# Row normalization on one core: the last scale is shared by two engines in both tiles, and the last store is issued on the ScalarE queue

## Chip, cores, metric

One Trainium2 chip, one core. The metric is device microseconds of a whole execution. All runs quoted here were in the fast state (granted clock 1.0); one program on one core.

## The reference

```python
def reference(x, axis, eps):          # x: (1024, 4096) float32, axis -1, eps 1e-12
    norm = np.sqrt(np.sum(x ** 2, axis=axis, keepdims=True) + eps)
    return (x / norm).astype(np.float32)
```

16.78 MB are read and 16.78 MB written; the arithmetic per element is one square, one add and one multiply.

## The kernel before

Each of two tiles holds 4 rows in each of 128 partitions (64 KiB per partition, contiguous in HBM). Both loads are issued at the start; each store follows its tile's scales. What the change and the argument touch:

```python
    def scale(self, r):
        self.nc.vector.tensor_scalar_mul(
            out=self.x[:, r], in0=self.x[:, r], scalar1=self.rstd[:, r : r + 1]
        )

    def scale_by_both(self, r):
        cut = 7 * self.D // 8
        rstd = self.rstd[:, r : r + 1]
        self.nc.scalar.activation(
            out=self.x[:, r, :cut], in_=self.x[:, r, :cut], func=ACT_F.Copy, scale=rstd,
        )
        self.nc.vector.tensor_scalar_mul(
            out=self.x[:, r, cut:], in0=self.x[:, r, cut:], scalar1=rstd
        )
# ... cut ...
    for i in range(n_tiles):                                   # n_tiles = 2
        g = RowGroups(nc, io, stats, scratch, D, R, eps_t)
        load = nc.sync.dma_start(out=g.flat(), in_=x_t[i])
        # ... cut: the first load is moved to the front ...
    for i, g in enumerate(groups):
        # ... cut: squares, norms and scales of rows 3, 0, 1; square of row 2 ...
        g.norm(2)
        if i < n_tiles - 1:
            g.scale_by_both(2)
        else:
            g.scale(2)
        store = nc.sync.dma_start(out=out_t[i], in_=g.flat())
    gpsimd_waits_for_last_store(nc, store.ins)
```

## Time and profile before

| | before |
|---|---|
| time, median (lowest to highest) | 81.92 us (81.86 to 81.96), 3 runs |
| profiled span | 80.2 us |
| VectorE / ScalarE busy | 26.7 / 29.7 us |
| DMA engines busy | 97.4% of the span, one queue |
| last store issued / landed | 56.76 / 80.03 us |

How to read it: a share near 100% on the DMA line and under 40% on the engines says that the end is set by bytes, not by arithmetic. To see whether a later or earlier issue matters, compare the issue time with the time at which the engines run out of the work queued ahead of it. The page and its stretches, timeline and chain are shown and read in the prediction below.

In the table of stretches, a DMA packet is counted whole, time and bytes, in the stretch in which it starts. So for a short stretch in which each of the 16 engines starts exactly one packet, "DMA share x length" is the mean duration of that packet, and "GB/s x length" is 1.05 MB (16 x 64 KiB). For the first packets of the last store, in the kernel before (columns: stretch, length, busy time and count of VectorE, ScalarE and GpSimd, clock, DMA share, GB/s):

```profile
59.70:60.40 0.70, 0.00 (x0) 0.00 (x0) 0.00 (x0) 1.00 3.47 1498
```

1498 x 0.70 = 1049 KB, all sixteen; 3.47 x 0.70 = 2.43 us per packet. The packet records themselves (start and duration of each) say 2.42.

### The profile page before, as it was taken

The page shows a single profiled execution, that of the slowest core. Times are in us where ns is not written, and L with a number is a line of the kernel's source. Part 1 is how long each engine was busy: PE and PEld are TensorE (multiplying, and loading weights), DVE is VectorE, ACT ScalarE, POOL GpSimd, SP SyncE. Part 2 cuts the span into 40 slices and gives each one's busy share as a digit, 9 for nine tenths or more (in the row PEclk, how much of TensorE's full clock was granted, in tenths as well). Part 3 has the DMA queues.
Part 4 walks back from the last instruction along what each step waited for, and adds up shares of the span by engine and source line. Part 5 has one row for each costly group of instructions (what it writes and reads, how often), then busy time and mean ns, then how long its engine had stood idle before and what let it go on. Part 6 is the DMA issues. An engine that isn't in the chain of part 4 may idle for free.

```text
span 80.2 us, 93 instructions
## 1 busy us (share of the span) xinstructions
DVE 26.7 (33%) x21; ACT 29.7 (37%) x23; POOL 0.2 (0%) x4
## 2 busy tenths in 40 slices
DVE  0000000000099599960039995999200000000000
ACT  6000000000099999989439999950000000000000
POOL 0000000000000000000000000000000000000000
DMA  9099996699996699996699990999991999992990
GB/s 490 33 523 523 523 490 294 261 523 523 523 490 261 294 523 523 523 490 261 294 523 523 523 490 33 523 523 523 523 458 65 523 523 523 523 425 98 523 523 0
DMA packets 576, 33.55 MB, mean 418 GB/s; under 512 B 64, under 2 KB 64, under 8 KB 64
## 3 DMA queue, kind: packets, MB, share of 16 engines
q1 hardware_dynamic: 576, 33.55, 97.4%
HBM read 16.78 MB, written 16.78 MB: 418 GB/s over the span
## 4 chain that ended last, share of the span: by engine, by line
DMA 51%; ACT 10%; DVE 9%; issue 0%
DMA xt<-in_x_dram 51%; ACT sq_act L33 9%; DVE xt L64 9%; ACT rstd L53 1%; DVE rstd L59 0%
## 5 line engine op out<-in xcount | busy, mean ns | idle before, releaser
L33 ACT ACTIVATE sq_act<-xt 128x4096 f32<-128x4096 f32 x6 | 21.7, 3609 | 22.4 <-DMA xt<-in_x_dram 22.4
L42 DVE SCALAR_TENSOR_TENSOR sq_dve<-xt 128x4096 f32<-128x4096 f32 x2 | 8.9, 4426 | 26.4 <-DMA xt<-in_x_dram 26.4
L64 DVE TENSOR_SCALAR xt<-xt,rstd 128x4096 f32<-128x4096 f32 x7 | 16.5, 2353 | 0.2
L72 ACT ACTIVATE xt<-xt,rstd 128x3584 f32<-128x3584 f32 x1 | 3.3, 3283 | 0.2 <-DVE rstd L59 0.2
L53 ACT ACTIVATE rstd<-ssq,eps_t 128x1 f32<-128x1 f32 x8 | 2.1, 290 | 0.1
L59 DVE RECIPROCAL rstd<-rstd 128x1 f32<-128x1 f32 x8 | 1.3, 160 | 2.5 <-ACT rstd L53 2.5
L33 ACT ACT_TABLE_LOAD x1 | 1.3, 1283 | 0.8 <-PEq L258 0.8
L53 ACT ACT_TABLE_LOAD x1 | 1.3, 1283 | 0.0
L33 ACT ACTIVATION_READ_ACCUMULATOR sq_act<-xt 128x1 f32 x6 | 1.1, 187 | 0.0
L78 DVE TENSOR_SCALAR xt<-xt,rstd 128x512 f32<-128x512 f32 x1 | 0.5, 487 | 0.0
L211 DVE MEMSET eps_t<- 128x1 f32 x1 | 0.1, 59 | 0.9 <-PEq L258 0.9
L42 DVE DVE_READ_ACCUMULATOR sq_dve<-xt 128x1 f32 x2 | 0.2, 83 | 0.0
L258 POOL MEMSET const-uint8-127<- 128x1 uint8 x1 | 0.1, 103 | 0.0
L258 POOL MEMSET const-bfloat16-1.0<- 128x1 bf16 x1 | 0.1, 102 | 0.0
L258 POOL MEMSET const-float32-0.0<- 128x1 f32 x1 | 0.1, 99 | 0.2 <-issue 0.2
L258 POOL MEMSET const-float32-1.0<- 128x1 f32 x1 | 0.1, 99 | 0.0
## 6 DMA issues: line engine op xcount, KB each, us to landing
xt<-in_x_dram SPq DMA_DIRECT2D x2, 31.3
out_dram<-xt SPq DMA_DIRECT2D x2, 22.5
```

The lines of the kernel that those rows point to most:

```text
L33: self.nc.scalar.activation(out=sq_a, in_=self.x[:, r], func=ACT_F.Square, accum_out=self.ssq[:, r : r + 1],)
L42: self.nc.vector.scalar_tensor_tensor(out=sq_v, in0=self.x[:, r], scalar=1.0, in1=self.x[:, r], op0=ALU.mult, op1=ALU.mult, accum_out=self ...
L53: self.nc.scalar.activation(out=self.rstd[:, r : r + n], in_=self.ssq[:, r : r + n], func=ACT_F.Sqrt, bias=self.eps_t,)
L59: self.nc.vector.reciprocal(out=self.rstd[:, r : r + n], in_=self.rstd[:, r : r + n])
L64: self.nc.vector.tensor_scalar_mul(out=self.x[:, r], in0=self.x[:, r], scalar1=self.rstd[:, r : r + 1])
L72: self.nc.scalar.activation(out=self.x[:, r, :cut], in_=self.x[:, r, :cut], func=ACT_F.Copy, scale=rstd,)
L78: self.nc.vector.tensor_scalar_mul(out=self.x[:, r, cut:], in0=self.x[:, r, cut:], scalar1=rstd)
L211: nc.vector.memset(eps_t, eps)
L258: nc = _bacc.Bacc("TRN2", target_bir_lowering=False, num_devices=1)
```

## The change

The intent, as far as the diff shows it: the same code for both tiles, with the last scale split between two engines, and the last store issued by the engine that has just finished the larger part of it.

```diff
-        if i < n_tiles - 1:
-            g.scale_by_both(2)
-        else:
-            g.scale(2)
-        store = nc.sync.dma_start(out=out_t[i], in_=g.flat())
+        g.scale_by_both(2)
+        queue = nc.sync if i < n_tiles - 1 else nc.scalar
+        store = queue.dma_start(out=out_t[i], in_=g.flat())
```

## The prediction

> **What bounds the kernel now.** I read the page's engine line and DMA rows first, then the busy table by stretches of time, then the timeline around the two stores, then the chain of work that ended last. All figures are of the kernel before; its span is 80.2 us, its time 81.92 us.
>
> The page's engine line, its rate row and its queue row:
>
> ```profile
> DVE 26.7 (33%) x21; ACT 29.7 (37%) x23; POOL 0.2 (0%) x4
> ...
> GB/s 490 33 523 523 523 490 294 261 523 523 523 490 261 294 523 523 523 490 261 294 523 523 523 490 33 523 523 523 523 458 65 523 523 523 523 425 98 523 523 0
> ...
> q1 hardware_dynamic: 576, 33.55, 97.4%
> ```
>
> No compute engine is busy for even 40% of the span, while the one DMA queue's packets fill 97.4% of what 16 DMA engines have. The ups and downs of the rate row are not pauses: a packet is counted whole in one slice. Of the 576 packets 64 are under 512 B (the completion marks), so 512 carry 64 KiB each, 32 per engine in turn: 8 for each of two loads and two stores. The queue's share gives about 0.974 x 80.2 x 16 / 512 = 2.44 us per packet; the DMA records of the trace say 2.42 us for nearly all of them, with about 2 ns between one packet of an engine and its next.
>
> The busy table by stretches, cut where a round of packets ends, shows the same (columns: stretch, its length, busy us and count of each engine, clock, DMA share, rate):
>
> ```profile
> 4.82:41.06 36.24, 12.45 (x10) 16.56 (x12) 0.00 (x0) 1.00 1.00 434
> 41.06:60.38 19.32, 14.23 (x10) 11.88 (x10) 0.00 (x0) 1.00 1.00 434
> 60.38:79.70 19.32, 0.00 (x0) 0.00 (x0) 0.00 (x0) 1.00 0.88 380
> 79.70:80.21 0.51, 0.00 (x0) 0.00 (x0) 0.00 (x0) 1.00 0.00 0
> ```
>
> The second stretch is store 0 draining, and all of tile 1's compute lies inside it. The third is store 1 draining, with no compute at all. (Its 0.88 is where packets are counted at their starts: the first ones of that store began just before the cut. 128 packets of 2.42 us over 16 engines are 19.36 us, the whole stretch.) The engine that starts last takes its first packet at 2.12 us and ends its last at 79.69: 77.57 us for 32 packets, 2.424 each. It never waits. The last landing is at 80.03 and the span ends at 80.20.
>
> So the end is set by 33.55 MB through 16 busy DMA engines, and the question for the change is only whether store 1 is ready before the engines run out of store 0. The timeline around the last scales and issues (start, us, engine, line):
>
> ```profile
> 35.48 0.16 DVE L59 RECIPROCAL rstd<-rstd 128x1 f32<-128x1 f32 x1 [0.57 <-ACT rstd L53]
> 35.68 3.28 ACT L72 ACTIVATE xt<-xt,rstd 128x3584 f32<-128x3584 f32 x1 [0.23 <-DVE rstd L59]
> 35.68 0.49 DVE L78 TENSOR_SCALAR xt<-xt,rstd 128x512 f32<-128x512 f32 x1
> 38.99 0.35 SPq L240 DMA_DIRECT2D out_dram<-xt  x1
> ...
> 54.18 0.16 DVE L59 RECIPROCAL rstd<-rstd 128x1 f32<-128x1 f32 x1
> 54.38 2.35 DVE L64 TENSOR_SCALAR xt<-xt,rstd 128x4096 f32<-128x4096 f32 x1
> 56.76 0.34 SPq L240 DMA_DIRECT2D out_dram<-xt  x1
> ```
>
> Tile 0 shows what the shared scale costs, tile 1 what the whole VectorE scale costs. Store 1 is issued at 56.76. In the DMA records, the sixteen engines finish store 0 between 59.79 and 60.37 and each goes on to store 1 2 ns later, so store 1 is already waiting. Lastly, the chain that ended last, whose final line is:
>
> ```profile
> 54.38 2.35 DVE xt L64
> ```
>
> It stops at 56.73, because this view follows compute and the final transfer has none behind it. The page's 9% for VectorE on this chain is therefore not time that can be won.
>
> **What the Trainium skill says.** "DMA: Bandwidth & Descriptors", section "Specifications", gives a fabric ceiling of 435 GB/s for the 16 engines. The trace agrees: 434 GB/s over the 55 us of stretches one and two. The same page, "Issuing engines are not separate DMA queues", says that DMAs from the scalar, sync or gpsimd engine run on the same 16 engines and interleave, and that issuing from several only saves sequencer time. Before, all issues are SyncE's, of 0.34 to 0.38 us each; no run yet shows ScalarE's. "ScalarE: Activation LUTs", section "Table sets: the hidden batching unit", says that cheap functions such as copy are filler in every set. The trace agrees: ScalarE's Copy at 35.68 follows Sqrt with no table load between them, and the only two loads are at 0.79 and 25.81.
>
> **The change, part by part.**
>
> 1. *The scale.* Removed: one VectorE scale of 128x4096, 2.353 us (54.377 to 56.730). Added: a VectorE scale of 128x512, 0.487 us, and a ScalarE Copy of 128x3584, 3.283 us, beside each other. Both need the reciprocal, which ends at 54.183 + 0.158 = 54.34. In tile 0 both began 0.035 us after it; here that gives 54.38. ScalarE is free by then (its last Sqrt ends at 53.34). VectorE's part ends at 54.38 + 0.49 = 54.86, ScalarE's at 54.38 + 3.28 = 57.66. The scale ends 57.66 - 56.73 = 0.93 us LATER than before. In tile 0 the split uses idle engines too, but the slow side gets seven eighths; it is no saving here.
>
> 2. *The issue.* Before, SyncE began its issue 0.027 us after VectorE's end (56.730 to 56.757). Now ScalarE waits for its own Copy; I take the same 0.03, so 57.69, an issue of about 0.35 us. ScalarE has nothing else to do, so its 0.35 us delays nothing. The order of the built kernel shows exactly these edits: ScalarE gains one Copy and one DMA, VectorE's last scale shrinks, SyncE loses one DMA, and no table load is added.
>
> 3. *From issue to the first byte.* Store 0 measures it: issued at 38.99, while the first engine had finished load 1 at 40.265 and stood idle until 40.475. So the first engine had its work 1.485 us after the issue, and the later ones by 40.67, 1.68 us after. For store 1: ready at 57.69 + 1.49 = 59.18 on the first engine, 57.69 + 1.68 = 59.37 on the last. The engines finish store 0 at 59.79 at the earliest. Slack before: 59.79 - (56.76 + 1.49) = 1.54 us. Slack after: about 0.6 us, or 0.4 by the slowest figure. [...]
>
> 4. *The transfer.* 128 packets of 2.42 us as before. With its own ring, store 1 may take turns with store 0's last packets from 59.2 on rather than line up behind them; the sum of bytes per engine is the same, so only store 0's landing (60.7 now) may shift, and nothing waits for it but a drain long before the end.
>
> 5. *The tail.* GpSimd waits for the last store's semaphore as before; 0.17 us from landing to end stays.
>
> Sum: +0.93 us (scale) - 0.93 us (absorbed in slack) + 0 (transfer) + 0 (tail) = 0. Predicted time 81.9 us.
>
> **The rivals.**
>
> *First, the slack does not hold (slower).* It needs an issue on ScalarE's own ring to take much longer than one on SyncE's. The very first load, with everything cold, needed 1.01 us for its first engine and 2.12 us for its last. Even 2.12 us gives 57.69 + 2.12 = 59.81, 0.02 us behind the earliest engine and before most of the others (the last needs it at 60.37). If the first DMA of ScalarE cost 1 us more than that, the loss would be about 0.5 us, 82.4. For 2% (1.64 us) it would have to be ready only at about 60.37 + 1.64 = 62.0, an issue-to-data time of over 4.3 us. Nothing in the profile speaks for that.
>
> *Second, two rings are better than one (faster).* If engines lost time at the seam between two stores on one ring, a second ring could fill it. Against it: the seam is 2 ns on every engine. And 434 GB/s over the whole middle leaves no hole for a second ring to fill. At most the 0.2 us hole at the load 1 to store 0 seam is in question, and the change doesn't touch that issue; the last engine doesn't have it either.
>
> *Third, two rings are worse.* Packets of two stores interleaving, or a second queue's set-up and clean-up around the kernel (81.92 - 80.2 = 1.7 us lie outside the profiled span), could cost some tenths: 82.1 to 82.4. No view of before can exclude this, since only one queue ran.
>
> **Range and chances.** The three runs before lie within 0.1 us, the profiled one took 82.04; another chip and the third rival add some tenths upward, and the second takes at most 0.3 off. So 81.6 to 82.4 for 8 in 10. Beyond 2% either way (under 80.3 or over 83.6) needs the DMA stream to shrink, which 77.57 us of unbroken packets forbid, or the over 4 us of issue latency: 1% for faster, 2% for slower.
>
> **What would show it right or wrong.** Right: the page shows a second queue with 144 packets and 8.39 MB beside 432 on the first, the two shares together near 97%; ScalarE's Copy at about 54.4 for 3.28 us; ScalarE's issue at about 57.7; the DMA share stays full through 59 to 61 us; the last landing at about 80.0. The chain of work ends with ScalarE's line, later than before, and the span doesn't move. Wrong: a hole in the DMA records around 60 us (the slack failed, step 3), packets other than 2.42 us while both queues have work (step 4), an unchanged span with a changed time (set-up of the second queue), or a last landing that moves for no hole at all.

## The result, and the profile after

The changed kernel took 82.72 us (82.59 to 82.83, 6 runs), the kernel before 81.93 us (81.73 to 81.96, 6 runs). The ratio is 1.0099, 95% interval 1.0085 to 1.0114: the mean time of one kernel's fast runs over that of the other's of the same rounds, so not quite the ratio of the medians. The change costs 0.8 us where the prediction had none. 82.72 lies above its range of 81.6 to 82.4 and clearly outside the noise; that the change would stay within 2% held.

The page's engine line, rate row and queue rows of the changed kernel:

```profile
DVE 24.9 (31%) x21; ACT 33.0 (41%) x24; POOL 0.2 (0%) x4
...
GB/s 518 0 518 518 518 518 486 97 453 518 518 518 486 162 389 518 518 518 518 0 518 518 518 518 453 130 453 518 518 518 0 518 518 518 518 130 389 518 518 0
...
q1 hardware_dynamic: 432, 25.17, 72.9%
q10 hardware_dynamic: 144, 8.39, 24.9%
```

VectorE lost 1.8 us and ScalarE gained 3.3, as foreseen. There is a second queue, q10, with the 128 large packets of the last store and its 16 marks. The queue rows already give the loss away. On q1, 0.729 x 80.9 x 16 / 384 = 2.46 us per large packet; on q10, 0.249 x 80.9 x 16 / 128 = 2.52. Eight packets per engine, each 0.1 us above 2.42 on average, are 0.8 us: the whole loss. (On q1 it is mostly the first packets of the first load that lift the mean.) The two shares still add up to 97.8%, so there is no idle hole; something took longer.

The timeline around the last scale and the issue, and the last line of the chain of work:

```profile
54.09 0.15 DVE L59 RECIPROCAL rstd<-rstd 128x1 f32<-128x1 f32 x1
54.28 0.49 DVE L78 TENSOR_SCALAR xt<-xt,rstd 128x512 f32<-128x512 f32 x1
54.28 3.28 ACT L72 ACTIVATE xt<-xt,rstd 128x3584 f32<-128x3584 f32 x1 [1.04 <-DVE rstd L59]
57.59 0.37 ACTq L238 DMA_DIRECT2D out_dram<-xt  x1
```

```profile
54.28 3.28 ACT xt L72
```

The compute side is as predicted: Copy at 54.28 for 3.28 us, issue at 57.59. The chain ends with ScalarE's line, at 57.56. The surprise is in the stretch where the engines pass from store 0 to the last store:

```profile
59.70:60.50 0.80, 0.00 (x0) 0.00 (x0) 0.00 (x0) 1.00 4.08 1311
```

Again all sixteen start here (1311 x 0.80 = 1049 KB), but 4.08 x 0.80 = 3.26 us each, against 2.43 before. In the packet records each of them starts 2 ns after the end of an engine's last packet of store 0, between 59.85 and 60.31, and lasts 3.07 to 3.48 us; the next round is back at 2.42. So each engine stood 0.65 to 1.06 us, 0.84 on average, "inside" its first packet of the new queue. Nothing else of that size differs: an engine's packets sum to 78.09 us on average before and to 79.14 after. Of this 1.05 us more, 0.84 lie in this round and about 0.2 in the last rounds of load 1 (2.46 to 2.50 us a packet; no other profile of the set has these long rounds, so they are this one execution's and not the change's). The first packets of all began 0.16 us earlier, which takes some of it back.

What could make it so? There were four theories:

- **Later scale**: the slack was not there after all; the 0.93 us later scale costs directly.
- **Cold queue**: the first use of ScalarE's queue is slow.
- **Slow issue**: a ScalarE issue always needs some 3.2 us until data flows (57.59 to 60.75).
- **Change of ring** (the "ring" of a queue is here the row of packets that it has waiting for an engine): passing from one queue's ring to the other's costs the engine a start-up, as if its pipeline had run empty. The first packets of the whole kernel have the same look (3.15 us on average in this run, against 2.42 in the round after), which is why I thought of it.

### The profile page after: what moved, and what is told of

It reads as the page before. It is cut to its first block, busy times and chain, and to the rows that moved or that the text cites. A ratio compares the mean times of both kernels' runs of the same rounds, so it can differ in the third digit from the quotient of the medians.

```text
span 80.9 us, 94 instructions
## 1 busy us (share of the span) xinstructions
DVE 24.9 (31%) x21; ACT 33.0 (41%) x24; POOL 0.2 (0%) x4
## 4 chain that ended last, share of the span: by engine, by line
DMA 50%; ACT 14%; DVE 6%; issue 0%
DMA xt<-in_x_dram 50%; ACT sq_act L33 9%; DVE xt L64 6%; ACT xt L72 4%; ACT rstd L53 1%; DVE rstd L59 0%
## 5 line engine op out<-in xcount | busy, mean ns | idle before, releaser
L64 DVE TENSOR_SCALAR xt<-xt,rstd 128x4096 f32<-128x4096 f32 x6 | 14.1, 2353 | 0.2
L72 ACT ACTIVATE xt<-xt,rstd 128x3584 f32<-128x3584 f32 x2 | 6.6, 3283 | 1.3 <-DVE rstd L59 1.3
L78 DVE TENSOR_SCALAR xt<-xt,rstd 128x512 f32<-128x512 f32 x2 | 1.0, 486 | 0.1
```

Source lines behind the costliest of these rows:

```text
L64: self.nc.vector.tensor_scalar_mul(out=self.x[:, r], in0=self.x[:, r], scalar1=self.rstd[:, r : r + 1])
L72: self.nc.scalar.activation(out=self.x[:, r, :cut], in_=self.x[:, r, :cut], func=ACT_F.Copy, scale=rstd,)
L78: self.nc.vector.tensor_scalar_mul(out=self.x[:, r, cut:], in0=self.x[:, r, cut:], scalar1=rstd)
```

## The experiments

The whole set, three rounds each, every result correct. The rounds ran on several chips, so the ratio, taken within the same rounds, says more than the time. "Issued" is the start of the last store's issue; "first packet" the mean of the 16 first packets of the last store.

| run | last store on | issued | first packet | time us | ratio to before |
|---|---|---|---|---|---|
| changed kernel | ScalarE | 57.59 | 3.26 | 82.72 | 1.010 |
| e1 scale only | SyncE | 57.6 | 2.42 | 81.90 | 0.999 |
| e2 queue only | ScalarE | 56.55 | 2.42 | 81.83 | 0.998 |
| e3 warmed queue | ScalarE | 57.45 | 3.26 | 82.76 | 1.010 |
| e4 both stores | ScalarE | 57.70 | 2.42 (store 0: 2.96) | 82.73 | 1.009 |
| e5 even split | ScalarE | 55.83 | 2.42 | 81.84 | 1.000 |
| e6 share 2816 | ScalarE | 56.85 | 2.90 | 82.41 | 1.007 |
| e7 share all | ScalarE | 57.76 | 3.26 | 82.67 | 1.010 |
| e8 late VectorE | ScalarE | 57.38 | 3.26 | 82.61 | 1.010 |
| e9 short last packet | ScalarE | 57.72 | 2.42 | 82.17 | 1.0035 |
| e10 its control | SyncE | 56.48 | 2.42 | 81.96 | 1.001 |
| e11 rings swapped | SyncE | 57.53 | 2.46 (store 0: 3.25) | 82.72 | 1.011 |
| e12 short first packet | ScalarE | 57.52 | 1.60 for 20 KiB | 82.73 | 1.010 |

### First four: halves of the change, a warmed queue, both stores

**e1**, the changed kernel with the store back on SyncE:

```diff
-        queue = nc.sync if i < n_tiles - 1 else nc.scalar
+        queue = nc.sync
```

> Only the shared last scale, last store still issued by SyncE. All theories that blame the new queue (first packet on a new ring is slow; ring switch costs; ScalarE's issue is slow to reach the engines) expect the time of the kernel before, about 81.9 us, with the last round-24 packets at 2.42 us, because the issue at about 57.7 plus 1.5 us still comes before 59.8. The rival that the 0.93 us later scale itself is what costs (the slack was not there) expects about 82.7 us and a hole in the DMA records near 60 us.

("Round 24" are the first packets of the last store, with rounds of sixteen counted from 0.) 81.90 us, ratio 0.9991 (0.9972 to 1.0009), first packets 2.70 x 0.90 = 2.43 us:

```profile
59.50:60.40 0.90, 0.00 (x0) 0.00 (x0) 0.00 (x0) 1.00 2.70 1165
```

The later scale is free, as the prediction's slack said. "Later scale" is out. In the records, the sixteen last packets of store 0 begin between 0.48 us before and 0.28 us after the issue at 57.61, much as in the changed kernel (0.16 before to 0.30 after). So at the same lateness every engine pays on the other ring and none on its own.

**e2**, the kernel before with the last store on ScalarE's queue:

```diff
-        store = nc.sync.dma_start(out=out_t[i], in_=g.flat())
+        queue = nc.sync if i < n_tiles - 1 else nc.scalar
+        store = queue.dma_start(out=out_t[i], in_=g.flat())
```

> Only the ScalarE queue; the last scale stays whole on VectorE, so ScalarE issues at about 56.8 instead of 57.6. Fixed cost theory (the first packet of each engine on a ring other than the last one takes 3.25 us instead of 2.42): 82.7 us, as the changed kernel. Readiness theory (a ScalarE issue needs about 3.2 us to data, seen as 57.6 to 60.8): data at about 60.0, so loss of at most 0.2 us, 82.0 us.

81.83 us, ratio 0.9984 (0.9968 to 0.9999). Each half of the change is free, and both together cost 0.8 us. The stretch of the first packets, and the issue:

```profile
56.55 0.37 ACTq L241 DMA_DIRECT2D out_dram<-xt  x1
```

```profile
59.50:60.30 0.80, 0.00 (x0) 0.00 (x0) 0.00 (x0) 1.00 3.04 1311
```

3.04 x 0.80 = 2.43 us: a change of ring at full speed. So the change of ring alone is not the cost either, nor is it a fixed price. What differs from the changed kernel is that the issue came one microsecond earlier.

**e3**, the changed kernel with a small DMA on ScalarE's queue at the start:

```diff
+    warm = scratch_pool.tile([16, 128], F32)
+    nc.scalar.dma_start(out=warm, in_=x[0:16, 0:128])
```

> The changed kernel plus one tiny DMA (16 rows of 512 B, 8 KB, read and never used) issued by ScalarE at the start. Cold-ring theory (only the first use of ScalarE's ring is slow): the last store's first packets take 2.42 us and the time falls to about 81.9 to 82.0. Switch theory (any change of ring on an engine empties the pipeline): the last store still pays 0.84, and the tiny DMA may pay once more, 82.7 to 83.5.

82.76 us, first packets 3.26 us (4.09 x 0.80 in its stretch): "cold queue" is out. The small DMA brought something better than its purpose. Its row among the DMA issues:

```profile
warm<-in_x_dram ACTq DMA_DIRECT2D x1, 8.0 KB, 8.9
```

8 KB took 8.9 us to land. In the packet records, on every engine, it ran between the second and the third packet of load 0 (from 6.40 us on), although it was issued at 0.78, 0.2 to 0.5 us before the first packets began. And it ran without any gap: 27 ns for its 512 B, and the next packet of load 0 began at once. An engine seems to settle its next packet one packet ahead.

**e4**, both stores on ScalarE:

```diff
-        queue = nc.sync if i < n_tiles - 1 else nc.scalar
+        queue = nc.scalar
```

> Both stores issued by ScalarE, shared scale in both tiles. Switch theory: one change of ring, now between load 1 and store 0, costs about 0.84, and store 1 follows store 0 on the same ring at 2.42: 82.7 us. Readiness theory with 3.2 us from issue to data: store 0 issued at about 38.9 has data at 42.1 against 40.3 to 41.0 needed, so a loss of about 1.4 us: 83.3 us.

82.73 us. The last store, issued by ScalarE as late as 57.70 but behind store 0 on the same ring, has first packets of 2.42 us, the earliest from 59.84 on, so "slow issue" is out: a ScalarE issue doesn't always need 3.2 us. (Ten engines got there some 0.5 us late and so prove little; the other six began their last packets of store 0 between 0.31 us before and 0.07 us after the issue, and paid nothing.) The change of ring is now between load 1 and store 0, and there the sixteen engines fall into two kinds:

```profile
40.20:41.10 0.90, 0.00 (x0) 0.00 (x0) 0.00 (x0) 1.00 3.30 1165
59.80:61.15 1.35, 0.00 (x0) 0.00 (x0) 0.00 (x0) 1.00 1.80 777
```

The first row averages to 2.97 us, the second to 2.43. In the records behind the first row, the ten packets that start 2 ns after a packet of load 1 (engine still busy when store 0's work came) last 3.09 to 3.49 us. The six that start after a pause (engine already out of work) last 2.45 to 2.46. An engine that stands idle takes up the other ring without the long packet (its pauses here, 0.20 us on average, are shorter too); one that is busy with its last packet does not.

After these four I changed the theory: what counts is how early the other ring's work arrives, before the engines run out. I called it the lead theory.

### Moving the issue time

Three variants of the last tile's split set the time of ScalarE's issue (n = 1536, 2816 and 4096 for e5, e6, e7; for e7 the empty VectorE part is left out):

```diff
-    def scale_by_both(self, r):
-        cut = 7 * self.D // 8
+    def scale_by_both(self, r, cut):
...
-        g.scale_by_both(2)
+        g.scale_by_both(2, 7 * D // 8 if i < n_tiles - 1 else n)
```

**e5**, n = 1536. 

> The changed kernel, but in the last tile ScalarE scales only 1536 of 4096 columns and VectorE the rest, about 1.6 us each, so that ScalarE issues the last store at about 55.9 instead of 57.6. Lead theory (the change of ring costs about 0.84 us only if the new ring's work comes later than some 2.7 to 3.0 us before the engines run out of the old ring's): free, about 81.9 us, first packets of the last store 2.42 us. If a Copy on ScalarE in front of its own DMA were the cause: 82.7 us.

81.84 us, ratio 1.0000 (0.9985 to 1.0015), first packets 3.03 x 0.80 = 2.42 us. This is the changed kernel with its cost removed:

```profile
59.50:60.30 0.80, 0.00 (x0) 0.00 (x0) 0.00 (x0) 1.00 3.03 1311
```

It doesn't beat the kernel before: both are at the DMA limit.

**e6**, n = 2816.

> The same with 2816 columns on ScalarE: issue at about 56.95, 2.65 us before the first engine and 3.2 us before the last engine runs out of store 0, between the free case (56.55) and the costly one (57.45). Lead theory: this is near the edge, some engines pay (first packet about 3.2 us) and some do not, and the slowest engine decides: 81.9 or 82.7 us.

82.41 us, ratio 1.0068 (1.0053 to 1.0083): on the edge. The two halves of the round, by start time:

```profile
59.60:59.80 0.20, 0.00 (x0) 0.00 (x0) 0.00 (x0) 1.00 7.29 2294
59.80:60.20 0.40, 0.00 (x0) 0.00 (x0) 0.00 (x0) 1.00 3.63 1475
```

2294 x 0.20 / 65.5 = 7 packets of 7.29 x 0.20 x 16 / 7 = 3.33 us; 9 packets of 3.63 x 0.40 x 16 / 9 = 2.58. In the records, the seven engines that run out of store 0 first all pay (3.20 to 3.47 us); of the other nine, two pay and seven do not (2.418 us exactly). So it is decided engine by engine, and it is all or nothing. The engines that began their last packet of store 0 up to 0.52 us after the issue (56.85) paid, those that began it 0.68 us or more after did not; between the two it is mixed (two free at 0.55 and 0.57, two paying at 0.59 and 0.65).

**e7**, n = 4096.

> The same with all 4096 columns on ScalarE (no VectorE part): issue at about 58.0, 0.4 us later than in the changed kernel. Lead theory (a fixed price for a change of ring found too late): no dearer than the changed kernel, 82.7 us, data still 0.7 to 1.1 us after each engine runs out. Readiness theory (a fixed time of about 3.2 us from the issue): 0.4 us more, 83.1 us.

82.67 us: no dearer than the changed kernel, though ScalarE's Copy is 0.43 us longer. (The table shows the issue only 0.17 later because this profile runs earlier as a whole; against the starts of the last packets of store 0 it is 0.37 us later on average.) First packets again 4.08 x 0.80 = 3.26 us:

```profile
59.50:60.30 0.80, 0.00 (x0) 0.00 (x0) 0.00 (x0) 1.00 4.08 1311
```

The price does not grow with the delay, so it is not a wait for the issue.

**e8**, ScalarE's queue with the last scale on VectorE alone, made 0.9 us longer by eight pieces (cut: the last scale against the kernel before; the two lines of the queue are those of e2):

```diff
-            g.scale(2)
+            for c in range(0, D, 512):
+                nc.vector.tensor_scalar_mul(
+                    out=g.x[:, 2, c : c + 512],
+                    in0=g.x[:, 2, c : c + 512],
+                    scalar1=g.rstd[:, 2:3],
+                )
```

> ScalarE queue, and the last scale on VectorE alone as in the kernel before, but in eight pieces of 512 columns, which takes about 0.9 us longer: ScalarE issues at about 57.5 with no Copy of its own in front. Lead theory: 82.7 us with first packets of about 3.25 us, as the changed kernel. If the Copy in front of the issue were the cause: 81.9 us.

82.61 us, first packets 3.26 us. It is the time of the issue, not the Copy in front of it on the same engine.

### What the lead is measured against

Together e3, e4 and e6 suggest a sharper rule, the commit theory: an engine settles its next packet when it starts the present one. If the other ring's work is there by then, the change is free; if it comes while the last packet of the old ring runs, the engine finishes that packet and starts anew. Three runs test it.

**e9**, the changed kernel with store 0 in two parts, the last packets being a quarter of the size, and its control **e10**, the kernel before with the same split:

```diff
-        store = queue.dma_start(out=out_t[i], in_=g.flat())
+        if i < n_tiles - 1:
+            cut = (R - 1) * D
+            queue.dma_start(out=out_t[i][:, :cut], in_=g.flat()[:, :cut])
+            queue.dma_start(out=out_t[i][:, cut:], in_=g.flat()[:, cut:])
+        else:
+            store = queue.dma_start(out=out_t[i], in_=g.flat())
```

> The changed kernel (ScalarE issues the last store at about 57.5), but store 0 is issued as two DMAs on SyncE: three rows of each partition in packets of 48 KiB, then the fourth in packets of 16 KiB, so that each engine's last packet of the old ring lasts about 0.6 us instead of 2.42. Commit theory (the new ring's work is taken up without a gap only if it is there, about 0.55 us after the issue, before the engine starts its last packet of the old ring; the last packets now start at about 59.0 to 59.6): free, 81.9 us, first packets of the last store 2.42 us. If a fixed lead of about 3 us in time were needed whatever the packet: 82.7 us.

> Control: the kernel before with store 0 split in the same way, all on SyncE. Both theories: 81.9 us; if it is slower or faster, the split itself has a price or a gain that the run above must be corrected for.

In e9 the issue is at 57.72, about as late as in any run, but each engine's last packet of store 0 lasts 0.61 us and begins at 59.10 or later. All first packets of the last store take 2.42 us (the stretch has one packet of 16 KiB besides the sixteen of 64; without its 0.61 us the mean is (3.08 x 0.80 x 16 - 0.61) / 16 = 2.43):

```profile
57.72 0.37 ACTq L243 DMA_DIRECT2D out_dram<-xt  x1
```

```profile
59.70:60.50 0.80, 0.00 (x0) 0.00 (x0) 0.00 (x0) 1.00 3.08 1331
```

From the issue to the end of store 0 there are 1.99 us on the first engine and 2.74 on the last, and nobody pays; in e6 engines paid with 2.78 to 3.07. So no fixed lead in time fits both runs, while a lead counted from the start of the last packet does. One thing in the records does not fit the letter of the commit theory. If the new work were taken into account 0.65 us after the issue, and each engine settled its next packet then, taking the two queues in turn, the first packet of the last store would come before the last small one: every engine began two or three more of these after that time. On all sixteen it came after them. So 0.5 to 0.65 us is the edge that was measured with 64 KiB packets; that the choice falls exactly at the start of a packet is not shown.

The time is 82.17 us, ratio 1.0035 (1.0010 to 1.0059), not the 81.9 expected. The control has 81.96, ratio 1.0012 (0.9996 to 1.0028). The 0.84 is gone from the records, but some 0.2 us of the time are left that I can't place (the two intervals overlap, so even the 0.2 is not certain): in its profile the last engine starts load 0 at 2.16 us against 1.92 in the control's, which is 0.24, but one profile doesn't show that this is so in all four runs.

**e11**, store 0 on ScalarE and the last store on SyncE, so that rings change twice:

```diff
-        queue = nc.sync if i < n_tiles - 1 else nc.scalar
+        queue = nc.scalar if i < n_tiles - 1 else nc.sync
```

> Rings the other way round: loads on SyncE, store 0 issued by ScalarE, last store by SyncE, shared scale in both tiles, so two changes of ring, both with late work. Commit theory: at the first change the engines that were still busy with load 1 pay about 0.8 and the idle ones do not (as with both stores on ScalarE); at the second the work arrives at about 58.25, before the late ones start their last packet of store 0 (58.2 to 58.7: free) and after the early ones have (57.4 to 57.8: pay), so each engine pays once: about 82.7 us. If each late change cost every engine 0.84: 83.5 us. If only ScalarE's ring were slow: at the second change every first packet at 2.42 us, 82.7 us.

82.72 us. Here the engines were all still busy when store 0 came, and all paid at the first change (3.25 us on average). That made them late, and at the second change only one engine paid. The two rows are the engine that starts first, and the other fifteen:

```profile
60.40:60.50 0.10, 0.00 (x0) 0.00 (x0) 0.00 (x0) 1.00 1.91 655
60.50:61.00 0.50, 0.00 (x0) 0.00 (x0) 0.00 (x0) 1.00 4.55 1966
```

One packet of 1.91 x 0.10 x 16 = 3.06 us, fifteen of 4.55 x 0.50 x 16 / 15 = 2.43. The issue was at 57.53. The one that paid began its last packet of store 0 at 58.04, 0.51 us later; the next began at 58.12, 0.59 us later, and did not pay. Two late changes on every engine at 0.84 would have been 83.5 us. That one packet, 0.63 us too long, is the only sign in the set that a change to SyncE's ring has a price too; that ScalarE's queue as such is not slow is shown by e2, e5 and e9, where it costs nothing.

**e12**, the last store in two parts, small packets first:

```diff
-        store = queue.dma_start(out=out_t[i], in_=g.flat())
+        if i < n_tiles - 1:
+            store = queue.dma_start(out=out_t[i], in_=g.flat())
+        else:
+            cut = (R - 1) * D - 1024
+            queue.dma_start(out=out_t[i][:, cut:], in_=g.flat()[:, cut:])
+            store = queue.dma_start(out=out_t[i][:, :cut], in_=g.flat()[:, :cut])
```

> The changed kernel, but the last store is issued by ScalarE as two DMAs, first the last 5120 columns of each partition (packets of 20 KiB), then the other 11264 (44 KiB), both after its Copy. It asks what the price of the change of ring is made of. A start-up latency (as in the first packets of the very first load): the 20 KiB packets, about 0.76 us at the usual rate, take about 1.6 us, the price stays at 0.8 us and the time is 82.7 us. A price in proportion to the first packet's size (one packet moved at a lower rate): 0.84 x 20/64 = 0.26 us, first packets of about 1.0 us, 82.2 us.

82.73 us. The stretch of the first packets, and one of the second:

```profile
59.50:60.30 0.80, 0.00 (x0) 0.00 (x0) 0.00 (x0) 1.00 2.02 410
61.20:61.80 0.60, 0.00 (x0) 0.00 (x0) 0.00 (x0) 1.00 1.27 546
```

A 20 KiB packet takes 1.27 x 0.60 = 0.76 us in the second round and 2.02 x 0.80 = 1.62 in the first (1.60 by the records): 0.84 us more, the same as with 64 KiB. So it is a start-up time that does not depend on the packet's size, as far as these two sizes show.

## Why the prediction was wrong, point by point

- *What bounds the kernel*: right. All versions sit on a stream of packets of 2.42 us, and no version went more than 0.2% below the kernel before.
- *Step 1, the scale*: right. Copy 3.28 us; e1 shows that its 0.93 us are absorbed.
- *Step 2, the issue*: right; 57.59 against 57.69 foreseen.
- *Step 3, from issue to the first byte*: this is the step that failed. It took a readiness of 1.49 to 1.68 us from SyncE's ring, where store 0 followed load 1 on the same ring, and compared it with 59.79, when the engines run out. (One reading was slightly off: the packet at 40.475 follows at once on an engine that had just finished load 1, and the five engines that stood idle took theirs from 40.487 to 40.681, 1.50 to 1.69 us after the issue. That moves the slack by 0.01 us.) On the same ring the comparison is right: e1, and the last store of e4, lose nothing with issues at 57.6 and 57.7. For the other ring, what decided was where an engine **starts its last packet** of the old ring, not where it ends it. That is a whole packet (2.42 us) earlier: in the changed kernel the last packets start at 57.43 to 57.89. By e2, e6 and e11 an engine goes free if this start comes some 0.5 to 0.65 us or more after the issue. The issue would have had to come by about 56.8 to 56.9, my estimate from 57.43 less 0.5 to 0.65; it came at 57.59. The slack that step 3 put at +0.4 to +0.6 us was in truth about -0.7 us, and the price of missing it is a start-up of 0.84 us per engine on average, which did not grow with the delay (e7).
- *Step 4, the transfer, "128 packets of 2.42 us as before"*: wrong for the first round (3.26), right for the other seven. The text named this sign ("packets other than 2.42 us"), but gave it to packets taking turns, which isn't the mechanism.
- *Step 5, the tail*: right: landing at 80.77, end 0.18 us later.
- *The rivals*: the third ("two rings are worse, some tenths, 82.1 to 82.4; no view of before can exclude this") was the nearest, with the wrong reason and half the size. The second looked at the seam, where the prediction found 2 ns, but that was the seam within one ring.
- *Range*: the upper end of 82.4 allowed 0.5 us for an effect that the text itself said no view could exclude.

What stays open: why the start-up takes 0.65 to 1.06 us and why an idle engine (e4) shows almost none of it, neither in its packet (0.04 us) nor in the pause before it (0.20 us on average); at what moment an engine chooses its next packet (e9); and the last 0.2 us of e9.

## What to carry to other kernels

When transfers run back to back, moving one of them to another issuing engine's queue was free here only if it was issued some 0.65 us before the DMA engines began their last packet of the old queue; with packets of 64 KiB that is about 3 us before they run out. If the issue is late, stay on the queue that the engines are already working on, or make the last packets ahead of it small (in e9 this took the long first packets away; the time was still 0.35% above the kernel before). And the slack that was measured on one queue did not hold for a change to another.

## What the Trainium skill lacked or had wrong

- "DMA: Bandwidth & Descriptors", section "Issuing engines are not separate DMA queues", says that issuing from several engines only saves sequencer time. It does not say that it can cost: a late change from one queue to the other cost 0.84 us per engine (first packets of 3.26 us in place of 2.42), while the same issue time on the same queue cost nothing (e1, e4).
- The same page, section "Queues, rings and completion order", says that an engine alternates between queue rows at packet granularity. In e3 that is so: the 512 B of ScalarE's queue ran between two packets of load 0. In e9 no alternation shows: every engine began two or three more packets of 16 KiB later than 0.65 us after the issue on the other queue, and finished them first. The page doesn't say when the next packet is chosen: an 8 KB DMA issued at 0.78 us waited behind two packets until 6.40 us (e3), and in e6 and e11 an engine pays or not by whether its last packet began before or after some 0.5 to 0.65 us from the issue.
- No page has the start-up of an engine on a ring it was not on: 0.84 us on ScalarE's ring with packets of 64 KiB and of 20 KiB alike (e12); on SyncE's ring one engine alone met it, with 0.63 us (e11).
